# A four-layer decoder trunk on one core: the issue order of all five queues from a fixed table

## The chip, the core and the metric

The kernel runs on one core of a Trainium2 chip. The core has five instruction queues that run side by side and meet through semaphores: TensorE (PE) for matmuls and transposes, VectorE (DVE), ScalarE (ACT) and GpSimd (POOL) for elementwise work, and SyncE (SP), which here only issues DMAs. Each queue works through its instructions in the order in which the program has them; an instruction that waits holds everything behind it on its queue. The metric is device time in microseconds of one execution; the profile is one such execution, recorded instruction by instruction.

## What is computed

One sequence of 1024 positions, width 1024, goes through four layers, causal, all positions at once. The token mixers are, in order, HGRN2, sliding-window attention, gated DeltaNet and HGRN2 again:

```python
for i in range(DEPTH):
    j = i // N_MIXERS
    mod = (c @ ada_w[i] + ada_b[i])[:, None, :]
    shift, scale, gate = jnp.split(mod, 3, axis=-1)
    h = rmsnorm(x, norm_g[i]) * (1.0 + scale) + shift
    kind = i % N_MIXERS
    if kind == 0:
        y = hgrn2_mixer(h, hg_in_w[j], hg_out_w[j], hg_onorm[j], lb_all[i])
    elif kind == 1:
        y = swa_mixer(h, sw_in_w[j], sw_out_w[j], sw_qnorm[j], sw_knorm[j], sw_sinks[j], ang)
    else:
        y = gdn_mixer(h, gd_in_w[j], gd_out_w[j], gd_conv_w[j], gd_a_log[j], gd_dt_bias[j], gd_onorm[j])
    x = x + gate * y
```

Each mixer is an input projection of width 4096 (HGRN2), 2560 (attention) or 6176 (DeltaNet), a sequence part, a gate and an output projection. The sequence part of HGRN2 is a recurrence in chunks with one 128 x 128 state for each of 8 heads; attention looks back 128 positions with 16 heads; DeltaNet is a recurrence in chunks with 16 value heads, a triangular inverse for each chunk and a short convolution ahead of it. All is float32.

## The kernel before

Activations lie with the 1024 channels on partitions (8 blocks of 128) and the positions in two halves of 512. A float32 product is made of three matmuls of rounded parts: every tile is split into a high part and a remainder, and `mm3` issues high x high (L222), high x low and low x high (L223, L224). Weights come from memory in 256 KB tiles (`load_w`: DMA on SP, cast to the high part on ACT, L193, remainder on DVE, L194). These projection matmuls, 128 x 512 each, are most of PE's work; the tiles they fill in PSUM are called proj_ps, projw_ps, projt_ps and outp_ps, and few of them exist at a time (three, in DeltaNet two), so that ACT and DVE must empty one before it is filled again.

The mixers' sequence parts are chains of small matmuls with ACT or DVE steps between them:

- HGRN2 (`mix` in `hgrn2`): decayed products (lev_ps, L1125 and L1170), a transpose (kh_ps, L1192), then for each of four chunks the output (o_ps, L1202 and L1203) and the next state (s_ps, L1207, which DVE turns into hg_S). The first layer's last head ends in a transpose ot_ps (L1234).
- Attention (`mix` in `swa`): transposes of q (L1481), scores (s_ps, L1496 to L1498), softmax on ACT and DVE, transposes of the weights (pt_ps, L1519, copied by ACT to sw_pth) and the product with v (pv_ps, L1525).
- DeltaNet (`scan` in `gdn`): for each chunk of 128 positions the products of the state with k and q (ks_ps, L942 and L943), gd_y on DVE, w_ps (L953), its scaled copies gd_ws and gd_wg on ACT (L954, L968), S_ps (L958), the new state gd_S on DVE, and w_ps once more (L969). Beside it run the inverse (`inverse`, L790 to L899) and the projections of later heads, whose convolution (`conv`) empties proj_ps by ACT's L692 and L696; transposes of k, q and v (L711) follow, with sums of squares on ACT (L718).

What is issued when is not written out by hand. The functions are generators, and `weave` takes turns between several of them (a recurrence, the projections of later heads, the next layer's adaLN vectors), each in proportion to a total that is written beside it. From what it is given so the framework orders each queue when the program is closed, by priorities (`high_priority`, with offsets such as `PRH` or `BURST`), by data dependencies, and by its own estimate of when an operand is ready. `issue_after` and `tied` add single order edges.

## Time and profile before

| what | value |
| --- | --- |
| median of three runs | 2648.4 us |
| lowest and highest of them | 2642.19 and 2651.18 us |
| the profiled execution | 2641.07 us |
| its span, first to last instruction | 2639.2 us |
| mean granted clock of PE in it | 0.995 |
| memory traffic | 117 GB/s over the span |

The page of the profile gives the busy time of each engine over the span. Further views cut it into windows, list the instructions of one engine in order of time, and name what ended a wait. PE's records overlap: a projection matmul's record is about 0.39 us long where the next begins 0.23 us after it, so short waits of PE don't show as idle time.

### The profile page before, as it was taken

Reading aid. Unit: us, or ns where it says so; the run is one execution under the profiler, and the core shown is the slowest. Engines: PE = TensorE matmul, PEld = TensorE weight load, DVE = VectorE, ACT = ScalarE, POOL = GpSimd, SP = SyncE. Lnnn points to the kernel's source line nnn. Section 1 sums busy time; section 2 is a strip of 40 time slices with the busy share of each in tenths; the row PEclk is TensorE's granted clock in tenths of the full one; section 3 lists DMA queues with packets and bytes.
Section 4 is the critical chain, followed back from the end, with each engine's and each line's share of the span. In section 5 each row is a group of like instructions: output and inputs, shape, how many; then the busy total and the mean of one; then the engine's idle time right before and its main releaser. Section 6 shows DMA issues by size and latency. Waiting matters only on the chain.

```text
span 2639.2 us, 50831 instructions
## 1 busy us (share of the span) xinstructions
PE 2556.0 (97%) x18271; PEld 2037.9 (77%) x18271; DVE 2020.7 (77%) x5663; ACT 1328.6 (50%) x3478; POOL 162.2 (6%) x382
## 2 busy tenths in 40 slices
PE   7999999999999999999999999999999999999999
PEld 4777777788888867777777777778678877787777
DVE  5585789877797878868899999988776837368775
ACT  4343344543464655545666665666544434245452
POOL 0001000001000000101010101110221000000000
PEclk8999999999999999999999999999999999999999
DMA  7333343643233252434343444334585312122443
GB/s 261 96 114 105 109 144 114 192 129 126 66 105 104 71 163 95 141 98 117 104 113 100 110 117 116 81 98 103 181 248 171 116 49 81 46 85 64 144 136 117
DMA packets 393617, 312.06 MB, mean 118 GB/s; under 512 B 74979, under 2 KB 320150, under 8 KB 393366
## 3 DMA queue, kind: packets, MB, share of 16 engines
q1 hardware_dynamic: 380822, 267.92, 34.5%
q0 software_dynamic: 12544, 40.90, 4.9%
q8 instruction: 144, 2.36, 0.4%
q14 instruction: 107, 0.88, 0.1%
HBM read 247.84 MB, written 60.88 MB: 117 GB/s over the span
## 4 chain that ended last, share of the span: by engine, by line
PE 73%; DVE 14%; DMA 6%; ACT 4%; issue 3%; SPq 1%; POOL 0%; DVEq 0%; ACTq 0%; POOLq 0%
PE proj_ps L222 10%; PE proj_ps L224 10%; PE proj_ps L223 10%; PE outp_ps L224 5%; PE outp_ps L222 5%; PE outp_ps L223 5%; PE projw_ps L223 2%; PE projw_ps L222 2%; PE projw_ps L224 2%; DMA ada_w<-in_ada_w_dram 2%; DVE gd_tb L698 1%; DVE w_lo L194 1%; PE projt_ps L223 1%; PE projt_ps L224 1%; PE projt_ps L222 1%
## 5 line engine op out<-in xcount | busy, mean ns | idle before, releaser
L222 PE MATMUL proj_ps<-hhi,w_hi 128*128 128x512 f32 x1664 | 676.0, 407 | 3.6 <-ACT gd_tb L696 3.3
L223 PE MATMUL proj_ps<-hlo,w_hi 128*128 128x512 f32 x1664 | 672.1, 404 | 0.0
L224 PE MATMUL proj_ps<-hhi,w_lo 128*128 128x512 f32 x1664 | 671.3, 404 | 0.0
L222 PEld LDWEIGHTS proj_ps<-hhi,w_hi 128*128 128x128 f32 x1664 | 314.7, 189 | 64.2 <-ACT gd_tb L696 5.9
L224 PEld LDWEIGHTS proj_ps<-hhi,w_lo 128*128 128x128 f32 x1664 | 314.4, 189 | 58.2 <-issue 0.4
L223 PEld LDWEIGHTS proj_ps<-hlo,w_hi 128*128 128x128 f32 x1664 | 315.0, 189 | 55.1 <-issue 0.9
L193 ACT CAST w_hi<-w_raw 128x512 fp32r<-128x512 f32 x356 | 216.7, 612 | 264.9 <-PE proj_ps L223 148.7
L194 DVE TENSOR_TENSOR w_lo<-w_raw,w_hi 128x512 fp32r<-128x512 f32 x356 | 239.1, 676 | 143.3 <-ACT w_hi L193 139.8
L222 PE MATMUL outp_ps<-o_hi,w_hi 128*128 128x512 f32 x576 | 228.3, 397 | 1.1 <-DVE x L1356 1.1
L223 PE MATMUL outp_ps<-o_lo,w_hi 128*128 128x512 f32 x576 | 228.7, 397 | 0.5 <-DVE o_lo L1331 0.4
L224 PE MATMUL outp_ps<-o_hi,w_lo 128*128 128x512 f32 x576 | 227.8, 396 | 0.5 <-DVE w_lo L194 0.5
L196 ACT ACTIVATE w_hi<-w_raw,par 128x512 fp32r<-128x512 f32 (+1 forms) x136 | 94.8, 697 | 141.6 <-PE outp_ps L223 95.0
L698 DVE SCALAR_TENSOR_TENSOR gd_tb<-gd_xs,taps,gd_tb 128x512 f32<-128x512 f32 x192 | 145.8, 759 | 16.3 <-ACT gd_tb L696 12.5
L448 DVE SCALAR_TENSOR_TENSOR ada_acc<-ada_w,par,ada_acc 128x512 f32<-128x512 f32 x154 | 115.0, 746 | 21.7 <-DMA ada_w<-in_ada_w_dram 20.9
L197 DVE SCALAR_TENSOR_TENSOR w_lo<-w_raw,par,w_hi 128x512 fp32r<-128x512 f32 (+1 forms) x136 | 96.8, 715 | 42.7 <-ACT w_hi L196 42.2
L222 PEld LDWEIGHTS outp_ps<-o_hi,w_hi 128*128 128x128 f32 x576 | 108.6, 189 | 24.7 <-issue 2.9
L223 PEld LDWEIGHTS outp_ps<-o_lo,w_hi 128*128 128x128 f32 x576 | 108.6, 189 | 23.4 <-DVE o_lo L1331 1.6
L224 PEld LDWEIGHTS outp_ps<-o_hi,w_lo 128*128 128x128 f32 x576 | 108.5, 188 | 22.9 <-DVE w_lo L194 1.0
L1322 POOL DMA_DIRECT2D o_in<-od x72 | 38.9, 541 | 1194.5 <-DVE sw_zs L1465 334.0
L222 PE MATMUL projw_ps<-w_hi,hhi 128*128 128x512 f32 x256 | 102.5, 406 | 2.4 <-DVE hg_q L1041 2.4
L223 PE MATMUL projw_ps<-w_lo,hhi 128*128 128x512 f32 x256 | 103.5, 406 | 0.3 <-DVE w_lo L194 0.3
L224 PE MATMUL projw_ps<-w_hi,hlo 128*128 128x512 f32 x256 | 102.2, 400 | 0.0
(429 smaller groups left out, 5360.1 us busy)
## 6 DMA issues: line engine op xcount, KB each, us to landing
ada_w<-in_ada_w_dram SPq DMA_DIRECT2D x160, 256.0 KB, 2.8
w_raw<-in_hg_in_w_dram SPq DMA_DIRECT2D x148, 256.0 KB, 2.8
w_raw<-in_gd_in_w_dram SPq DMA_DIRECT2D x128, 256.0 KB, 3.0
o_in<-od POOLq DMA_DIRECT2D x72, 256.0 KB, 3.6
x<-xd SPq DMA_DIRECT2D x64, 256.0 KB, 4.7
w_raw<-in_gd_out_w_dram SPq DMA_DIRECT2D x64, 256.0 KB, 3.3
xd<-x POOLq DMA_DIRECT2D x48, 256.0 KB, 2.8
w_raw<-in_sw_in_w_dram SPq DMA_DIRECT2D x44, 256.0 KB, 2.9
```

Of the source, the lines that this page charges most:

```text
L193: nc.scalar.copy(hi, raw)
L194: nc.vector.tensor_tensor(lo, raw, hi.bitcast(F32), ALU.subtract)
L196: nc.scalar.activation(hi, raw, AF.Copy, scale=scale)
L197: nc.vector.scalar_tensor_tensor(lo, raw, scale, hi.bitcast(F32), ALU.mult, ALU.subtract)
L222: mm(out, a[0], b[0], start=start, stop=False)
L223: mm(out, a[0], b[1], start=False, stop=False)
L224: mm(out, a[1], b[0], start=False, stop=stop)
L448: self.step = self.nc.vector.scalar_tensor_tensor(acc, w, c, acc, ALU.mult, ALU.add)
L698: last = nc.vector.scalar_tensor_tensor(y, xs[:, j:j + HT], w(j), y, ALU.mult, ALU.add)
L1322: nc.gpsimd.dma_start(t, od[(k0 + k) * P:(k0 + k + 1) * P, sl])
```

## The change

A table gives the order of all five queues. `trunk` calls `in_order` as its last step, when all instructions have been written down. For each queue the table holds, in compressed form, which of the instructions left is the next one; `in_order` ties each instruction to the one that the table puts ahead of it on its queue by an order edge, which asks for no wait. Priorities then have nothing left to decide. The table was worked out beforehand with longer hand-overs between engines. Operations, tiles and buffers are the same; only ACT gets two table loads more (8 for 6), which the compiler places where two functions of different tables follow each other.

```diff
+import base64
+import zlib
...
+ORDER = {
+    "PE": (
+        "c-rlo>2nmv6~N!FW>>qqZwawlohu2nI*?!`ap*z<gySF)?1(!7a~KHm2jU2m3J`<{kV>4wI1q4Ta8+W5xSVoTlFzB6Dqr#~Uy}SM`INk)dv>"
...
+    "Activation": (
...
+    "DVE": (
...
+    "SP": (
...
+    "Pool": (
...
+}
+
+
+def in_order(tc):
+
+
+    rest = {}
+    for i in tc.nc.cur_bb.bb.instructions:
+        if type(i).__name__ not in ("BassTilePoolBoundary", "InstRegisterMove"):
+            rest.setdefault(i.engine, []).append(i)
+    for e, table in ORDER.items():
+        left, places, last = rest[getattr(mybir.EngineType, e)], iter(zlib.decompress(base64.b85decode(table))), None
+        for n in places:
+            i = left.pop(n if n < 255 else next(places) + 256 * next(places))
+            if last is not None:
+                how = mybir.DependencyInfo(mybir.DependencyClass.NoSync, mybir.DependencyReason.DATA)
+                tc.add_manual_dep(i, last, how, reason="order")
+            last = i.name
+        assert not left
...
+    in_order(tc)
```

The new lines shift the kernel's line numbers by 128: L222 of before is L350 in rows of the change, L953 is L1081, and so on. On PE, 31% of the instructions keep their place, half move by at most 4 places and nine in ten by at most 25. On SP 51% keep theirs and none moves by more than 19; on POOL none by more than 8.

**First place: PE in the first HGRN2 layer, last head** (about 495 us in the profile of before), where the first chunk's output and state begin. Rows are line, operation, tile written <- tiles read, size. Before:

```order
L1192 MATMUL kh_ps<-ident,hg_kg 128x128 x4
L1203 MATMUL o_ps<-hg_v_513,hg_at_506 128x128
L1207 MATMUL s_ps<-hg_v_513,hg_kht 128x128
L1202 MATMUL o_ps<-hg_S,hg_qf 128x128
L1203 MATMUL o_ps<-hg_v_513,hg_at_506 128x128
L1207 MATMUL s_ps<-hg_v_513,hg_kht 128x128
L224 MATMUL proj_ps<-hhi,w_lo 128x512
```

The same first s_ps and the o_ps that needs its state, in the change:

```order
L1335 MATMUL s_ps<-hg_v_513,hg_kht 128x128
L351 MATMUL proj_ps<-hlo,w_hi 128x512
L352 MATMUL proj_ps<-hhi,w_lo 128x512
L350 MATMUL proj_ps<-hhi,w_hi 128x512
L351 MATMUL proj_ps<-hlo,w_hi 128x512
L352 MATMUL proj_ps<-hhi,w_lo 128x512
L1330 MATMUL o_ps<-hg_S,hg_qf 128x128
L1331 MATMUL o_ps<-hg_v_513,hg_at_506 128x128
L1335 MATMUL s_ps<-hg_v_513,hg_kht 128x128
```

Where o_ps stood right behind the s_ps whose state it needs, five projection matmuls now stand between the two.

**Second place: PE in DeltaNet's recurrence** (about 1293 us), where w_ps, S_ps and ks_ps of one head pair follow each other. Before:

```order
L953 MATMUL w_ps<-gd_y,gd_uq 128x128
L222 MATMUL proj_ps<-hhi,w_hi 128x512
L223 MATMUL proj_ps<-hlo,w_hi 128x512
L224 MATMUL proj_ps<-hhi,w_lo 128x512
L958 MATMUL S_ps<-gd_ws,gd_kt 128x256
L969 MATMUL w_ps<-gd_wg,gd_uq 128x128
L222 MATMUL proj_ps<-hhi,w_hi 128x512
L223 MATMUL proj_ps<-hlo,w_hi 128x512
L224 MATMUL proj_ps<-hhi,w_lo 128x512
L969 MATMUL w_ps<-gd_wg,gd_uq 128x128
```

In the change the same chunk, from the step ahead of it to the next projection matmul:

```order
L1086 MATMUL S_ps<-gd_ws,gd_kt 128x256
L1097 MATMUL w_ps<-gd_wg,gd_uq 128x128 x2
L1070 MATMUL ks_ps<-gd_S,gd_k 128x256
L1071 MATMUL ks_ps<-gd_S,gd_q 128x256
L1081 MATMUL w_ps<-gd_y,gd_uq 128x128 x2
L1086 MATMUL S_ps<-gd_ws,gd_kt 128x256
L1097 MATMUL w_ps<-gd_wg,gd_uq 128x128 x2
L1070 MATMUL ks_ps<-gd_S,gd_k 128x256
L1071 MATMUL ks_ps<-gd_S,gd_q 128x256
L350 MATMUL proj_ps<-hhi,w_hi 128x512
```

Two steps' worth of the recurrence, twelve instructions, now stand together, and the projection matmuls that stood between them stand ahead and behind.

**Third place: ACT in DeltaNet** (about 1396 us), around the sums of squares of q's transposes and the L696 that empties proj_ps. Before:

```order
L949 ACTIVATE gd_qse<-ks_ps,gd_ed 128x128
L718 ACTIVATE gd_tb,gd_ms<-qtr_ps 128x128 x4
L954 ACTIVATE gd_ws<-w_ps,gd_gw 128x128
L968 ACTIVATE gd_wg<-w_ps,gd_gm 128x128
L696 ACTIVATE gd_tb<-proj_ps,taps 128x512
L968 ACTIVATE gd_wg<-w_ps,gd_gm 128x128
```

In the change:

```order
L1082 ACTIVATE gd_ws<-w_ps,gd_gw 128x128
L832 ACTIVATE gd_tb<-gd_tb 128x512
L1096 ACTIVATE gd_wg<-w_ps,gd_gm 128x128 x2
L846 ACTIVATE gd_tb,gd_ms<-qtr_ps 128x128 x4
L824 ACTIVATE gd_tb<-proj_ps,taps 128x512
L1105 ACTIVATE gd_sq,gd_oms<-gd_ot 128x128 x2
```

The four sums (L718, now L846) moved behind gd_ws and both gd_wg, and L696 (now L824) stands right behind them. On PE the q transposes moved from nine rows ahead of the projection matmul that needs this L696 to four rows ahead.

## The prediction

> **What bounds the kernel now.** I read the page first: the busy shares, then the chain that ended last.

> ```profile
> span 2639.2 us, 50831 instructions
> ...
> PE 2556.0 (97%) x18271; PEld 2037.9 (77%) x18271; DVE 2020.7 (77%) x5663; ACT 1328.6 (50%) x3478; POOL 162.2 (6%) x382
> ...
> PE 73%; DVE 14%; DMA 6%; ACT 4%; issue 3%; SPq 1%; POOL 0%; DVEq 0%; ACTq 0%; POOLq 0%
> ```

> TensorE (PE) is busy for 2556.0 of 2639.2 us, and most of the chain is its own matmuls. Every PE instruction stays, so the order can only change the time that PE spends waiting: 83 us are seen as idle. So the next view is busy time by stage, in windows that I cut where the PE instructions of one layer give way to those of the next: set-up, first HGRN2 layer, attention, DeltaNet (GDN), second HGRN2 layer.

> ```profile
> core 0: us, PE busy (x) PEld busy (x) DVE busy (x) ACT busy (x) POOL busy (x), PEclk, DMA share, GB/s
> 0.00:57.00 57.00, 40.82 (x148) 21.52 (x149) 32.60 (x104) 22.67 (x40) 1.12 (x8) 0.88 0.83 302
> 57.00:520.00 463.00, 447.52 (x3921) 353.80 (x3922) 343.76 (x1083) 199.28 (x506) 14.74 (x52) 0.99 0.41 122
> 620.00:990.00 370.00, 361.26 (x2472) 301.64 (x2473) 287.81 (x826) 194.06 (x488) 6.50 (x12) 1.00 0.31 98
> 1240.00:1860.00 620.00, 604.73 (x4481) 484.88 (x4479) 563.71 (x1641) 395.65 (x1255) 54.73 (x138) 1.00 0.41 107
> 2130.00:2510.00 380.00, 375.79 (x3407) 298.12 (x3406) 247.88 (x869) 159.08 (x425) 2.17 (x4) 1.00 0.27 84
> ```

> Window length less PE busy gives the idle time: 16.2 us in the set-up, 15.5 and 4.2 in the two HGRN2 windows, 8.7 in attention, 15.3 in GDN. VectorE (DVE) is busy for 563.71 of 620 us in GDN (91%) and for 74%, 78% and 65% in the other three. There is little spare on DVE in GDN, and more elsewhere.

> The last view is the timeline of PE, for the price of one hand-over: PE writes PSUM, ACT or DVE reads it and writes SBUF, and a later matmul needs that. First a covered one, then an uncovered one (a plain fp32 matmul leaves two records, x2).

> ```profile
> 1285.78 0.39 PE L969 MATMUL w_ps<-gd_wg,gd_uq 128*128 128x128 f32 x2
> 1285.92 0.47 PE L222 MATMUL proj_ps<-hhi,w_hi 128*128 128x512 f32 x1
> 1286.23 0.39 PE L223 MATMUL proj_ps<-hlo,w_hi 128*128 128x512 f32 x1
> 1286.45 0.40 PE L224 MATMUL proj_ps<-hhi,w_lo 128*128 128x512 f32 x1
> 1286.76 0.49 PE L969 MATMUL w_ps<-gd_wg,gd_uq 128*128 128x128 f32 x2
> ...
> 1883.51 0.38 PE L969 MATMUL w_ps<-gd_wg,gd_uq 128*128 128x128 f32 x2
> 1884.35 0.49 PE L969 MATMUL w_ps<-gd_wg,gd_uq 128*128 128x128 f32 x2 [0.46 <-ACT gd_wg L968]
> ```

> With three projection matmuls between the two L969, the second starts 0.98 us after the first and nothing idles. With none it starts 0.84 us after it. The first occupies PE for 0.14 (1285.78 to 1285.92), so 0.70 us of PE time is lost. A projection matmul takes 0.22 to 0.31 (1285.92, 1286.23, 1286.45); I take 0.23. So a hand-over loses **0.70 us with no projection matmul in between, 0.47 with one, 0.24 with two and nothing with three**. Only part of it shows as idle, since records overlap (0.39 long, 0.23 apart).

> **The change, part by part.** The five queues hold the same instructions on the same buffers in another order; ACT has two table loads more. So each term is a count of hand-overs times that price. For every matmul of the mixers that waits for ACT or DVE, I followed its wait back in both orders to the last PE instruction that it needs, and counted the projection matmuls between the two.

> *HGRN2, both layers.* Matmuls with none, one or two in between: 16, 6 and 56 before; 7, 2 and 19 now. The first place of the section on the change is one of them. Before: 16 x 0.70 + 6 x 0.47 + 56 x 0.24 = 27.4 us. Now: 4.9 + 0.9 + 4.6 = 10.4. The change is **-17**. The same place shows a dearer hand-over, through DVE:

> ```profile
> 495.60 0.49 PE L1207 MATMUL s_ps<-hg_v,hg_kht 128*128 128x128 f32 x2
> 496.64 0.46 PE L1202 MATMUL o_ps<-hg_S,hg_qf 128*128 128x128 f32 x2 [0.56 <-DVE hg_S L1210]
> ```

> From 495.60 to 496.64 are 1.04 us, so 0.90 less the matmul's 0.14; at 0.90, 0.67 and 0.44 the same counts give 43.0 and 16.0, a gain of 27. The other end is nothing, if what releases these matmuls simply arrives later. I keep 0 to -27 and take 17, because it agrees with the 19.7 us of idle time in the two windows.

> *The longest single wait of that stage.*

> ```profile
> PE ot_ps L1234 <- DVE hg_tmp L1230: 2.8, 1, 2.8
> ...
> 508.00:511.50 3.50, 2.87 (x9) 2.52 (x10) 1.85 (x4) 1.32 (x3) 0.00 (x0) 0.51 0.19 56
> ```

> PE waits 2.8 us for hg_tmp, and the granted clock in the 3.5 us behind it is 0.51, so about 1.7 us more is lost there. In the new order six more projection matmuls stand ahead of that transpose, 6 x 0.23 = 1.4 us. That leaves a wait of 1.4 and, I assume, a clock that stays up: **-3** (0 to -4.5).

> *Attention.* 8, 7 and 2 before; 2, 4 and 5 now. 9.4 us before, 4.5 now: **-5** (0 to -9, the idle time of its window).

> *GDN.* Here the count goes the other way: 33, 20 and 17 before; 55, 16 and 29 now. 36.6 us before, 53.0 now: **+16**. Two patterns make it, shown at the second and third place of the section on the change. The first: chunk steps of the recurrence (L942, L943, L953, L958, L969) that follow each other with no projection matmul between. Runs of five or more such instructions: one of 13 before, in and around the window 1876 to 1884 us, and six now, of 12, 5, 8, 12, 6 and 14. The one of before shows what a run is:

> ```profile
> 1880.52 0.49 PE L953 MATMUL w_ps<-gd_y,gd_uq 128*128 128x128 f32 x2 [1.36 <-DVE gd_y L948]
> ...
> 1876.00:1884.00 8.00, 4.67 (x23) 3.22 (x22) 4.41 (x11) 5.47 (x20) 1.60 (x3) 1.00 0.29 94
> ```

> PE is busy for 4.67 of 8 us there. What waits behind the waiting instruction on PE are the projection matmuls of the next heads; ACT's and DVE's convolutions wait for these. The second pattern is on ACT:

> ```profile
> 1396.29 0.28 ACT L718 ACTIVATE gd_tb<-qtr_ps 128x128 f32<-128x128 f32 x1 [0.35 <-PE qtr_ps L711]
> ...
> 1397.06 0.29 ACT L718 ACTIVATE gd_tb<-qtr_ps 128x128 f32<-128x128 f32 x1
> ...
> 1397.81 0.73 ACT L696 ACTIVATE gd_tb<-proj_ps,taps 128x512 f32<-128x512 f32 x1
> ```

> A projection matmul that starts a new PSUM tile needs L696, which empties that tile, and L696 stands behind four L718 that need the transposes of q. The four take about 1.0 us (three steps from 1396.29 to 1397.06 are 0.77), L696 0.73. Of the L222 that wait for an L696, four had up to three projection matmuls of cover before, and ten have now. Six more at up to 1.5 us would be +9; I take none of it beyond the count, since some of these waits stand behind another wait that already lets ACT catch up. The bounds of GDN are 0 (PE would wait elsewhere in a stage where DVE is 91% busy) and +40, worked out under the rivals.

> *Table loads.*

> ```profile
> L1038 ACT ACT_TABLE_LOAD x3 | 3.8, 1283 | 0.1
> ```

> The second rope sine (L394) now stands behind sigmoids and squares, so its table is loaded again: 2 x 1.28 us on ACT, in the first HGRN2 window, where ACT is busy for 199 of 463 us and its casts run ahead of PE. Taken as 0 (0 to +2.6, if a gate that PE waits for stands behind a load).

> *DMA queues.* About half of SP's instructions keep their place and none moves by more than 19; GpSimd's move by 8 at most.

> ```profile
> PE ada_row L432 <- DMA ada_w<-in_ada_w_dram: 6.4, 2, 5.5
> ...
> w_raw<-in_gd_in_w_dram SPq DMA_DIRECT2D x128, 256.0 KB, 3.0
> ```

> PE's long wait for a transfer is that of the set-up, where the order hardly changes; the weight tiles, landing in 3.0 us, are issued ahead. Taken as 0 (-3 to +3).

> **Sum.** -17 - 3 - 5 + 16 = **-9 us**. The profiled execution took 2641.1 us (its span and 1.9 around it) and would take 2632. It lies 7.3 below the median of the three runs, 2648.4, so on the median's scale the forecast is **2639**, 0.35% less. About 0.3% (8 us) is what a measurement of this kernel can tell from no change, so this forecast lies at the edge.

> **Rivals.**

> *GDN gets the upper hand: slower.* The uncovered runs wait for DVE as at 1880.52 (1.36 us) rather than 0.70, because gd_y stands behind the inverse and the convolutions in DVE's own order. The 22 new uncovered hand-overs then cost 22 x 0.66 = 15 us more, and the six L222 the 9 us above: GDN +40. With -25 elsewhere that is +15, **2663**. It decides once GDN costs over 33. For: DVE's 91%. Against: in such a run PE feeds DVE nothing new, so DVE should catch up.

> *GDN costs nothing.* PE's waits there only change places, since DVE sets the pace: -25, **2623**. For: the same 91%. Against: PE is busy for 604.73 of 620 us too, and what it loses in a run it has no spare time to regain.

> *Nothing changes.* The 28 us of idle time in HGRN2 and attention is given back because the releasing ACT and DVE instructions moved back as well: **2648**. Against: the places shown have the matmuls moved by more than the wait.

> *The clock drops in the new runs.* Five new runs with one stretch of 3.4 us at half clock each, as behind 508 us, cost 5 x 1.7 = 8.5 us: **2647**. Against: the clock is 1.00 in 1876 to 1884 although PE idles for 3.3 of 8 us. [...]

> **How the numbers follow.** The forecast gets 0.45: its terms are rough, so 0.24 of it is faster by over 0.3%, 0.17 within, 0.04 slower. GDN for nothing 0.17, all faster. Nothing changes 0.12, all within. The clock 0.06, within but for 0.01 slower. GDN upper hand 0.20: 0.17 slower, 0.03 within. Together 0.41 faster, 0.37 within 0.3%, 0.22 slower. The range goes from 2616 (GDN free and HGRN2 at nearly 27) to 2664 (the slower rival), which leaves about a tenth out on each side.

> **What would show it.** In the changed profile, idle PE time in the first HGRN2 window should fall from 15.5 to about 6 us, in attention from 8.7 to about 5, and in GDN rise from 15.3 to some 25 or 30. In GDN's timeline the six runs should show S_ps, w_ps and ks_ps with idle time before them, released by gd_ws, gd_wg, gd_S and gd_y. If HGRN2 stays at 15, the hand-over count was the wrong measure; if GDN stays at 15, DVE sets its pace; if the granted clock falls in GDN, the last rival holds.

## Result and profile after

The changed kernel takes 2628.20 us (median of 4 runs, 2624.95 to 2630.06), the kernel before 2646.53 beside it (4 runs, 2642.19 to 2651.18). The ratio is **0.9929, 95% interval 0.9908 to 0.9950**, 18 us less. A second measurement, among the experiments, gave 0.9935 (0.9917 to 0.9954). The forecast was 2639 with a range from 2616 to 2664. On the scale of the profiled executions it was 2632; the profiled execution of the change took 2630.06 us, of which the span is 2628.4.

The page of the changed kernel: span, busy times, and the chain that ended last by engine.

```profile
span 2628.4 us, 50793 instructions
...
PE 2542.7 (97%) x18271; PEld 2058.0 (78%) x18271; DVE 2014.9 (77%) x5663; ACT 1328.7 (51%) x3480; POOL 164.7 (6%) x382
...
PE 80%; DVE 7%; DMA 6%; issue 4%; ACT 3%; SPq 0%; POOL 0%; DVEq 0%; ACTq 0%; POOLq 0%
```

VectorE's share of the chain has halved (14% before), TensorE's has grown from 73 to 80%: less of the span hangs on a hand-over. Busy time by stage, in the same windows as before (length, then busy time and records of each engine, granted clock, DMA share, GB/s):

```profile
0.00:57.00 57.00, 41.96 (x150) 22.89 (x151) 32.55 (x104) 23.06 (x41) 1.11 (x8) 0.84 0.84 302
57.00:520.00 463.00, 450.68 (x3960) 359.97 (x3960) 347.11 (x1094) 204.14 (x515) 14.77 (x52) 0.99 0.41 125
620.00:990.00 370.00, 366.50 (x2510) 311.17 (x2509) 289.48 (x830) 197.52 (x494) 6.61 (x13) 0.99 0.32 100
1240.00:1860.00 620.00, 592.08 (x4208) 483.41 (x4208) 548.51 (x1599) 386.79 (x1234) 53.52 (x132) 0.99 0.39 101
2130.00:2510.00 380.00, 378.71 (x3472) 304.45 (x3471) 254.19 (x885) 163.97 (x438) 3.24 (x6) 1.00 0.28 88
```

Idle TensorE time (length less busy) goes from 15.5 to 12.3 us in the first HGRN2 window, from 8.7 to 3.5 in attention, from 4.2 to 1.3 in the second HGRN2 window, and in GDN from 15.3 to **27.9**. The windows are fixed in time and the stages have moved in them, so I also took the start of every PE instruction in both traces (they are the same instructions) and the median difference, change less before, in stretches of 30 us: -10.3 us at 540, -20.3 at 1200, +1.0 at 1920, -10.9 at 2610. Stage by stage that is **-10 in the first HGRN2 layer, -10 in attention, +21 in GDN, -12 from there to the end**. For GDN the windows can be cut at the same instructions, which gives 5065 PE records in both (before, then the change):

```profile
1220.12:1940.10 719.98, 698.89 (x5065) 558.39 (x5064) 641.22 (x1805) 457.54 (x1426) 81.06 (x187) 1.00 0.44 118
1199.30:1941.10 741.80, 704.69 (x5065) 573.91 (x5064) 645.84 (x1820) 456.23 (x1426) 83.68 (x187) 0.98 0.42 114
```

The stage is 21.8 us longer. 16.0 us of it is idle time (21.1 to 37.1), and 5.8 us is longer busy time of the same matmuls.

The waits of TensorE on the instructions of GDN (us in total, times, longest), of the kernel before and then of the change (its lines are 128 higher: L696 is now L824, L953 is L1081):

```profile
PE proj_ps L222 <- ACT gd_tb L696: 3.3, 4, 1.5
...
PE S_ps L958 <- ACT gd_ws L954: 1.4, 3, 0.6
PE w_ps L953 <- DVE gd_y L948: 1.4, 1, 1.4
...
PE w_ps L969 <- ACT gd_wg L968: 1.2, 2, 0.8
```

```profile
PE proj_ps L350 <- ACT gd_tb L824: 9.9, 10, 1.6
...
PE proj_ps L350 <- DVE gd_tb L918: 4.8, 2, 2.4
PE w_ps L1081 <- DVE gd_y L1076: 3.9, 5, 0.9
...
PE S_ps L1086 <- ACT gd_ws L1082: 3.0, 6, 0.6
...
PE w_ps L1097 <- ACT gd_wg L1096: 2.6, 6, 0.6
PE w_ps L1081 <- ACT gd_ws L1082: 2.5, 5, 0.5
PE ks_ps L1070 <- DVE gd_S L1092: 2.3, 3, 1.2
```

Both patterns of the prediction are there: the waits of the recurrence, and the projection matmul behind L696, with the ten places that were counted; it is now the largest of TensorE's waits. A third one has come up that the prediction did not have: a projection matmul waits for a step of the inverse on VectorE (L918, which is L790 of before, where the wait is 0.2), 2.3 us ahead of GDN and 2.4 in it, at 1222 us. One of the six crowded runs in the change's timeline (start, length, engine, line, tile; idle time before it and what ended it):

```profile
1280.30 0.49 PE L1097 MATMUL w_ps<-gd_wg,gd_uq 128*128 128x128 f32 x2 [0.61 <-ACT gd_wg L1096]
1280.63 0.60 PE L1070 MATMUL ks_ps<-gd_S,gd_k 128*128 128x256 f32 x2
1281.06 0.59 PE L1071 MATMUL ks_ps<-gd_S,gd_q 128*128 128x256 f32 x2
1282.58 0.49 PE L1081 MATMUL w_ps<-gd_y,gd_uq 128*128 128x128 f32 x2 [0.92 <-DVE gd_y L1076]
1283.53 0.49 PE L1081 MATMUL w_ps<-gd_y,gd_uq 128*128 128x128 f32 x2 [0.46 <-ACT gd_ws L1082]
1284.47 1.22 PE L1086 MATMUL S_ps<-gd_ws,gd_kt 128*128 128x256 f32 x2 [0.46 <-ACT gd_ws L1082]
```

S_ps takes 1.22 us here and 0.70 elsewhere (x2 records, 1278.78): the clock has halved. The windows around it, cut where the clock changes:

```profile
1281.09:1284.50 3.41, 1.57 (x8) 0.79 (x6) 3.27 (x12) 2.18 (x9) 0.00 (x0) 1.00 0.41 103
1284.50:1291.33 6.83, 6.31 (x16) 4.99 (x17) 5.79 (x19) 3.58 (x17) 0.00 (x0) 0.50 0.17 42
```

TensorE is busy for 1.57 of 3.41 us, never idle for more than 0.92 us in one go, and the next 6.83 us run at half clock. The prediction had given this a chance of 0.06.

Why runs of this kind arise can be read from the number of projection matmuls between the ks_ps pair and the w_ps that waits for gd_y (the cover of that wait), for chunk steps 4 to 7 of the first and third head groups (u=0 and u=2):

```
              step 4   step 5   step 6   step 7
before  u=0      3        6        2        4
change  u=0      5       35        0        7
before  u=2      5       16        9       16
change  u=2      5       39        0       16
```

In the change VectorE's queue has 7.4 us of other work (the inverse, norms, transposes, convolutions) between the ks_ps pair of step 5 and its gd_y; the table covers this wait with 35 to 39 projection matmuls, and none are left for step 6.

### The profile page after: what moved, and what is told of

The parts are those of the page before. It is cut to its first block, busy times and chain, and to the rows that moved or that the text cites. A ratio compares the mean times of both kernels' runs of the same rounds, so it can differ in the third digit from the quotient of the medians.

```text
span 2628.4 us, 50793 instructions
## 1 busy us (share of the span) xinstructions
PE 2542.7 (97%) x18271; PEld 2058.0 (78%) x18271; DVE 2014.9 (77%) x5663; ACT 1328.7 (51%) x3480; POOL 164.7 (6%) x382
## 4 chain that ended last, share of the span: by engine, by line
PE 80%; DVE 7%; DMA 6%; issue 4%; ACT 3%; SPq 0%; POOL 0%; DVEq 0%; ACTq 0%; POOLq 0%
PE proj_ps L350 12%; PE proj_ps L351 12%; PE proj_ps L352 12%; PE outp_ps L350 4%; PE outp_ps L351 4%; PE outp_ps L352 4%; PE projw_ps L352 2%; PE projw_ps L351 2%; PE projw_ps L350 2%; DMA ada_w<-in_ada_w_dram 2%; PE projt_ps L350 2%; PE projt_ps L351 2%; PE projt_ps L352 2%; PE lev_ps L1253 1%; PE pv_ps L1653 1%
## 5 line engine op out<-in xcount | busy, mean ns | idle before, releaser
L350 PE MATMUL proj_ps<-hhi,w_hi 128*128 128x512 f32 x1664 | 677.0, 407 | 16.4 <-ACT gd_tb L824 9.9
L350 PEld LDWEIGHTS proj_ps<-hhi,w_hi 128*128 128x128 f32 x1664 | 315.2, 190 | 80.2 <-ACT gd_tb L824 15.6
L350 PE MATMUL outp_ps<-o_hi,w_hi 128*128 128x512 f32 x576 | 228.4, 398 | 1.6 <-ACT o_hi L1458 1.0
L350 PEld LDWEIGHTS outp_ps<-o_hi,w_hi 128*128 128x128 f32 x576 | 108.7, 189 | 25.0 <-issue 2.5
L350 PE MATMUL projw_ps<-w_hi,hhi 128*128 128x512 f32 x256 | 101.6, 402 | 2.4 <-DVE hg_q L1169 2.3
## 6 DMA issues: line engine op xcount, KB each, us to landing
ada_w<-in_ada_w_dram SPq DMA_DIRECT2D x160, 256.0 KB, 2.8
w_raw<-in_hg_in_w_dram SPq DMA_DIRECT2D x148, 256.0 KB, 2.9
w_raw<-in_gd_in_w_dram SPq DMA_DIRECT2D x128, 256.0 KB, 3.0
o_in<-od POOLq DMA_DIRECT2D x72, 256.0 KB, 3.6
x<-xd SPq DMA_DIRECT2D x64, 256.0 KB, 4.8
w_raw<-in_gd_out_w_dram SPq DMA_DIRECT2D x64, 256.0 KB, 3.2
xd<-x POOLq DMA_DIRECT2D x48, 256.0 KB, 2.7
w_raw<-in_sw_in_w_dram SPq DMA_DIRECT2D x44, 256.0 KB, 3.0
```

Of the source, the lines that this page charges most:

```text
L350: mm(out, a[0], b[0], start=start, stop=False)
```

## Experiments

Most of them mix the two orders. The order of before is written as a second table of the same form; the program is cut into pieces at places of the order of before, in all five queues at once and so that no piece needs a later one; within each piece either order is followed. TAKE names the pieces that follow the table of the change.

```diff
+TAKE = [0, 1, 3]
...
+def mixed(e):
+    now, was = places(ORDER[e]), places(WAS[e])
+    piece = {n: sum(k >= c for c in CUTS[e]) for k, n in enumerate(was)}
+    rank = {n: k for k, n in enumerate(now)}, {n: k for k, n in enumerate(was)}
+    return sorted(was, key=lambda n: (piece[n], rank[piece[n] not in TAKE][n]))
```

### Stage by stage

Cuts at 560, 1220 and 1940 us of the trace of before, which make four pieces: set-up with the first HGRN2 layer, attention, GDN, the second HGRN2 layer with the end.

All but GDN (TAKE = [0, 1, 3]):

> The order of the change in set-up, both HGRN2 layers and attention, the order of before in DeltaNet (GDN). By matching the same PE instructions in the two traces, the change gained about 10 us in the first HGRN2 layer, 10 in attention and 11 from the second HGRN2 layer to the end, and lost about 21 in GDN. Theory (each stage's gain and loss is its own): the 21 us of GDN stay away, so -31 us against before, about 1.2% (ratio 0.988). Rival (GDN starts earlier and then waits for something that the earlier stages do not bring nearer, so the loss is the earlier gain given back): GDN gives back 20 us in the old order too, ratio as the change's, 0.993 or nearer to 1.

GDN alone (TAKE = [2]):

> The order of the change in GDN alone, the order of before elsewhere. Theory: GDN's order costs what the two traces show there, +21 us (ratio 1.008), with idle PE time in the window of GDN up from 15 to about 28 us and the granted clock down to 0.5 for some stretches of 3.4 us. By the prediction's sum it would be +16 (1.006). Rival (gain given back): no gain ahead of it, so nothing to give back, 0 (ratio 1.000).

HGRN2 alone (TAKE = [0, 3]):

> The order of the change in set-up and in both HGRN2 layers (the second with what follows to the end), the order of before in attention and GDN. Theory: -21 us (ratio 0.992), idle PE time in the first HGRN2 window down from 15.5 to 12 us and in the second from 4.2 to 1.3. By the prediction's sum -20. Rival (hand-overs are no measure: what releases the matmuls comes later as well): within 0.2% of before.

Attention alone (TAKE = [1]):

> The order of the change in attention and the feed-forward behind it alone. Theory: -10 us (ratio 0.996), idle PE time in the attention window from 8.7 to some 4 us. By the prediction's sum -5 (0.998). Rival: 0, if the 10 us in the trace of the change were one execution's chance or came from starting earlier.

Measured, each against runs of before taken beside them (2644.86 us):

| order of the change in | ratio | 95% interval | us |
|---|---|---|---|
| all but GDN | 0.9899 | 0.9881 to 0.9918 | -26.7 |
| GDN alone | 1.0082 | 1.0069 to 1.0095 | +21.7 |
| HGRN2 alone | 0.9919 | 0.9905 to 0.9933 | -21.4 |
| attention alone | 0.9981 | 0.9969 to 0.9993 | -5.0 |

HGRN2 and GDN came out as the first theory said, and GDN costs 21.7 us with no gain ahead of it that could be given back, so its rival falls. All but GDN lies between its theory (0.988) and its rival (0.993), nearer to the theory; its interval holds neither. Attention gave 5 us, as the prediction's sum has it, not the 10 seen in place. And the three parts sum to -21.4 - 5.0 + 21.7 = -4.7 us, while the change makes -18: something is not additive. The same comparison of PE starts says where attention's other 5 us went: with its order alone the shift is -7.0 us at 1200 and -1.0 at 1260, at the entrance of GDN; in all but GDN it goes from -21.7 to -15.1 over the same place. There TensorE waits, in the kernel with all but GDN (its lines are 247 above those of before):

```profile
PE ktr_ps L958 <- DVE gd_k L952: 5.2, 1, 5.2
```

The kernel before waits 0.9 us for that tile. Attention's gain brings TensorE to the entrance earlier, and VectorE not by as much: with attention's order alone TensorE starts 6.9 us earlier than before at 1190 us and 7.0 at 1200, VectorE 4.3 and 1.7. To be early is not what costs: with HGRN2's order alone both engines are 5.6 us early at 1200, the wait for that tile is 1.1 us, and 5.4 us of the gain are still there at 1260. In all but GDN, VectorE's queue holds 17 short steps of the first inverse, 5 us in all, between the last two steps of the convolution that ends in gd_k (start, length):

```profile
1197.70 0.28 DVE L1092 TENSOR_TENSOR gd_tmp<-gd_A,gd_Tb 128x120 f32<-128x120 f32 x1
...
1202.45 0.22 DVE L1092 TENSOR_TENSOR gd_tmp<-gd_A,gd_Tb 128x56 f32<-128x56 f32 x1
1202.59 0.74 DVE L945 SCALAR_TENSOR_TENSOR gd_tb<-gd_xs,taps,gd_tb 128x512 f32<-128x512 f32 x1
...
1204.15 0.68 DVE L952 SCALAR_TENSOR_TENSOR gd_k<-gd_tb 128x512 f32<-128x512 f32 x1
```

### One crowded run, another seam, and the change again

Cuts at 1270 and 1940 us with the change outside (late cut, TAKE = [0, 2]); cuts at 1270 and 1320 us with the change inside (first run alone, TAKE = [1]); the change as it is.

> The order of the change in all that stands before 1270 us of the trace of before (set-up, first HGRN2 layer, attention, and the first 50 us of GDN) and again from 1940 us on, the order of before in between. The run with GDN left out as a whole, from 1220 us, lost 6 us at its seam: PE waited 3.4 us there, with 6.8 us at half clock behind it. Theory (that loss belongs to the seam, and GDN's order costs only from the first crowded run at 1305 us on): -33 us against before, ratio 0.9875. Rival (the old order of GDN needs what the old order ahead of it prepares, wherever the seam is): 0.990 again.

> The order of before, but for the piece from 1270 to 1320 us of its trace, which has the order of the change: the first of the six runs, 12 rows of the recurrence with no projection matmul between them. Theory: this one run carries the loss that the trace of the change shows there, +9 us (ratio 1.0035): 8 uncovered hand-overs x 0.70 = 5.6 us, and 6.8 us at half clock = 3.4. By the prediction's forecast, without the clock, +5.6 (1.002). Rival (PE's waits only change places within GDN, as DVE sets its pace): by the end of GDN the loss is made up, 1.000.

> The change itself once more, beside the runs of before of this call, since the three parts run one by one add up to -21.4 - 5.1 + 21.7 = -5 us and the change measured -18 with an interval of 11 us. Theory (stages add up but for what happens at the seams, some 6 to 10 us at the two ends of GDN): -10 to -15 us, ratio 0.995. Rival (the parts help each other): -18 or more, 0.993 or less.

Measured, against 2648.44 us: late cut **0.9910** (0.9891 to 0.9929), first run alone **1.0032** (1.0020 to 1.0045), the change **0.9935** (0.9917 to 0.9954).

The first run costs 8.5 us by itself (5.3 to 11.9), and the loss isn't made up later. The hand-overs with the clock (9) fit, but the 5.6 us without the clock lie inside the interval as well, and the trace of this run shows something that neither sum had: two waits behind L696, 2.2 us together, against 0.2 before in that stretch. So this run doesn't settle the clock's part. The late cut was a miss: it can't be told from all but GDN, and its PE starts lose as much at the entrance, ahead of its seam (-19.9 us at 1200, -14.1 at 1260). So the 6 us are no matter of the seam but of TensorE's being there ahead of VectorE. The change again is -17 us, so the parts do help each other, by some 13 us (with about 7 of uncertainty). From the PE starts, about half of that lies at the entrance: TensorE's lead costs 7 us there with the old order of GDN, the first run 9 us without that lead (3.6 to 12.8 us in GDN alone), and in the change both together cost 10 (-20.3 at 1200, -9.9 at 1380). The two losses overlap, in the same 100 us. The rest is no larger than the intervals allow for and stays open.

### The entrance of GDN

> The run with GDN left out (ratio 0.9899), with one place of TensorE's queue altered: the four ktr_ps transposes at GDN's entrance, which wait 5.2 us for gd_k at 1199 us, stand 19 projection matmuls (19 x 0.23 = 4.3 us) further back; the other four queues are as they were. Theory (attention arrives early and the wait at the entrance gives it back, since nothing is left ahead of those four): 4 us of the wait and the 3.4 us of the halved clock behind it go, -7 us, ratio 0.987. Rival (VectorE paces the entrance, so the wait turns up at the next matmul that needs VectorE): 0.990 as before.

```diff
         order = mixed(e)
+        if e == "PE":
+            order = [n for n in order if n not in [6842, 6843, 6844, 6845]]
+            k = order.index(6885) + 1
+            order[k:k] = [6842, 6843, 6844, 6845]
```

Measured **0.9878** (0.9853 to 0.9903) against 2648.70 us; all but GDN had 0.9899 (0.9881 to 0.9918), so the two can't be told apart. The waits in the same place say which theory holds:

```profile
PE qtr_ps L962 <- DVE gd_q L956: 4.3, 1, 4.3
PE ktr_ps L962 <- DVE gd_k L956: 1.2, 2, 0.9
```

The wait for gd_k fell from 5.2 us to 1.2 in two places, and 4.3 us turned up at the next transposes, which wait for gd_q. So the wait moves, as the rival says. That VectorE sets the pace is shown for gd_k, ahead of which its queue runs without a wait. Ahead of gd_q it has one:

```profile
1210.17 0.72 ACT L947 ACTIVATE gd_tb<-proj_ps,taps 128x512 f32<-128x512 f32 x1
...
1210.97 0.75 DVE L949 SCALAR_TENSOR_TENSOR gd_tb<-gd_xs,taps,gd_tb 128x512 f32<-128x512 f32 x1 [2.06 <-DMA tblk<-gd_Tb]
```

The convolution that ends in gd_q starts with L947 on ACT, which stands behind the copy and the sums of the very transposes that were moved back, and ends 0.08 us before VectorE's L949 starts; the profile puts the wait down to a transfer of the inverse that landed at the same time. Which of the two decided isn't shown. Either way, moving four instructions of TensorE's queue alone moved the wait and didn't end it.

### The clock

> The run with GDN's order alone, plus 15 matmuls whose results are never used (an fp32 128x128 by 256 columns each, 0.43 us in the trace): two ahead of the w_ps matmul that waits for gd_y in five chunk steps without a projection matmul, and one ahead of the second matmul that waits for gd_wg in five. They add no hand-over and take none away; they only keep TensorE busy while it waits, so that the 3.4 us around it are busy for over 0.65 instead of 0.46 to 0.55. Theory (half of GDN's +21.7 us is the halved clock behind such stretches): the two stretches of 6.8 and one of 3.4 us at half clock at 1310, 1904 and 1494 go, some 6 to 8 us, ratio 1.0055 against 1.0082. Rival (the clock plays no part; hand-overs and DVE do it all): the same 1.008, or slower by up to 15 x 0.43 = 6.5 us where the fillers stand in the way, 1.0105.

```diff
                     pks = self.psum("s", "ks_ps", 1)
+                    if (u, n) in FILL_W:
+                        FILL.setdefault(w1.ins.name, []).append(nc.tensor.matmul(pks[:, 0:256], dd["k"][hf][:, cs], dd["k"][hf][:, 0:256], start=True, stop=True).ins.name)
...
                 wg, ws = f256("wg"), f256("ws")
+                more = [nc.tensor.matmul(po[:, 256:512], dd["k"][hf][:, cs], dd["k"][hf][:, 0:256], start=True, stop=True).ins.name for _ in range(2 * ((u, n) in FILL_Y))]
```

Measured **1.0071** (1.0050 to 1.0091), against 1.0082 (1.0069 to 1.0095) without the fillers: inconclusive as a time. What they did to the waits and the clock isn't: TensorE's waits for gd_y went from 4.0 to 0.5 us and those for gd_wg from 2.6 to 0.6, and none of the stretches at half clock at 1310, 1494 and 1904 us is left. The filled step, with the two fillers (w_ps<-gd_k, x4) in place of a wait of 0.9 us:

```profile
1308.06 0.59 PE L1197 MATMUL ks_ps<-gd_S,gd_q 128*128 128x256 f32 x2
1308.49 1.03 PE L1205 MATMUL w_ps<-gd_k 128*128 128x256 f32 x4
1309.57 0.49 PE L1208 MATMUL w_ps<-gd_y,gd_uq 128*128 128x128 f32 x2
1310.52 0.49 PE L1208 MATMUL w_ps<-gd_y,gd_uq 128*128 128x128 f32 x2 [0.46 <-ACT gd_ws L1211]
```

The mean granted clock of the runs went from 0.9884 to 0.9900.

> The run with GDN left out (ratio 0.9899), plus 59 fp32 matmuls of 128x128 by 128 (the identity by itself, never used, about 0.14 us each) that fill four long waits of TensorE: 12 ahead of the matmul that waits 2.2 us for sw_zs at 606 us, 10 and 7 ahead of those that wait 1.9 us for mod and 1.3 us for sw_qhi at 930 to 934, 30 ahead of the four that wait 5.2 us for gd_k at 1199. They shorten no wait; they keep TensorE busy in it. Theory (a 3.4 us stretch in which TensorE is busy for less than about half halves the clock of the next): the stretches at half clock at 610, 934 and 1204 go, 1.7 + 3.4 + 3.4 = 8.5 us in the profiled execution of the run without them and some 6 in the mean, ratio 0.9875, granted clock up from 0.991 to 0.993 or more. Rival (the halved clock costs nothing there, or is set by something else than how busy TensorE is): 0.990, granted clock unchanged.

```diff
+WARM = {3325: ('s', 12), 5531: ('o', 10), 5539: ('o', 7), 6842: ('s', 30)}
...
+                pt = k.psum(tag, "warm_ps", 2 if tag == "lev" else 1)
+                FILL[n] = [mm(pt[:, 0:128], k.ident, k.ident, start=True, stop=True).ins.name for _ in range(count)]
```

Windows of all but GDN, cut at its clock changes, and the same windows with the fillers:

```profile
606.46:609.88 3.42, 1.26 (x8) 1.06 (x9) 2.06 (x4) 2.16 (x5) 0.00 (x0) 1.00 0.44 146
609.88:613.29 3.41, 3.41 (x19) 3.41 (x17) 1.59 (x3) 1.17 (x3) 0.00 (x0) 0.51 0.69 222
930.79:934.20 3.41, 0.60 (x4) 0.36 (x4) 2.46 (x8) 2.08 (x5) 0.42 (x1) 1.00 0.32 93
934.20:941.03 6.83, 6.72 (x23) 5.60 (x24) 5.71 (x14) 4.73 (x9) 2.36 (x6) 0.50 0.67 214
```

```profile
606.46:609.88 3.42, 3.42 (x33) 3.42 (x31) 2.08 (x3) 1.26 (x2) 0.03 (x1) 1.00 0.85 270
609.88:613.29 3.41, 3.18 (x26) 2.83 (x25) 2.64 (x5) 2.72 (x5) 0.00 (x0) 1.00 0.24 69
930.79:934.20 3.41, 3.41 (x28) 3.20 (x26) 0.62 (x2) 1.15 (x3) 0.00 (x0) 1.00 0.91 287
934.20:941.03 6.83, 5.89 (x44) 5.17 (x42) 5.90 (x16) 4.47 (x9) 2.15 (x4) 1.00 0.49 149
```

Matmuls that compute nothing of use took TensorE's busy time from 1.26 to 3.42 us in the stretch at 606.46 and from 0.60 to 3.41 in the one at 930.79, and the clock behind them is 1.00 where it was 0.51 and 0.50: in these two places it goes by how busy TensorE is. The mean granted clock rose from 0.9908 to 0.9935, which is 0.0027 x 2617 = 7 us less lost to it. The time is **0.9877** (0.9855 to 0.9898), against 0.9899 (0.9881 to 0.9918): 6 us better at face value, with an uncertainty of about 7, so no change isn't excluded. VectorE's queue is the same in both kernels, so its starts can be compared: relative to all but GDN the kernel with the fillers gains 1.1 us between 606 and 612 (expected 1.7), 1.2 between 928 and 960 (expected 3.4) and 1.4 at the entrance of GDN (expected 3.4), and gives up to 2.7 back within GDN. Of the 8.5 us expected, 3.7 came at the three places. That a halved clock costs its full price only where nothing but TensorE is late in what follows is my estimate from these numbers; it was not tried by itself.

> Both: the four ktr_ps transposes 19 projection matmuls further back, and the 29 fillers at 606 and 930 to 934. If both theories hold and add up: -7 from the entrance, -4 from the clock of the two other places, ratio 0.9855, about 38 us less than before. If only the entrance counts 0.987, if only the clock 0.988.

Measured **0.9881** (0.9859 to 0.9904): a miss. The two don't add up, nor is either told from all but GDN; the three kernels took 2618.49, 2617.76 and 2618.35 us and all but GDN 2618.91. All four beat both the kernel before and the change (by some 10 us, with 2628.20 and 2629.87 for the change), and the simplest, the order of the change everywhere but in GDN, is the version to keep.

## Why the prediction was right, and where it was not

| term | forecast, us | measured, us |
|---|---|---|
| HGRN2, with the wait for ot_ps | -17 - 3 | -21.4 (-25 to -18), alone |
| attention | -5 | -5.0 (-8 to -2), alone |
| GDN | +16 | +21.7 (18 to 25) alone, +8 to +10 beside the others (0.9929 and 0.9935 less 0.9899, each with some 7 us of uncertainty) |
| sum | -9 | -18 and -17 |

**HGRN2 held as a sum.** The count of uncovered hand-overs times 0.70, 0.47 and 0.24 us gave -17, and the wait for ot_ps (2.8 us before) is gone from the change's waits, with the half clock behind it (0.51 in 508.00 to 511.50 us before; 1.00 in the change from 62.50 to 612.05). No run takes single hand-overs apart, so the price is supported by the sum alone. The sign named for it didn't come: idle TensorE time in the first window was to fall to about 6 us and fell to 12.3, while the layer got 10 us shorter. The sign was at odds with the prediction's own price, of which only part shows as idle (0.46 of 0.70 us at 1884.35). The records in the window say it better: 3960 instead of 3921, 39 projection matmuls more, 39 x 0.23 = 9 us of work more in the same time.

**Attention held as a time**, as far as an interval of -8 to -2 can tell, by two errors of the count that cancel: the stage gains 10 us in place, and half is lost again at the entrance of GDN, where VectorE isn't ready. The prediction priced each stage by itself and had no term for what TensorE meets when it gets ahead of another engine.

**GDN was mis-sized, and its clock step was wrong.** The recurrence's count held: its waits show 11.5 us more idle time (5.9 to 17.4 in the groups of the page), and by the row at 1884.35 the 22 new uncovered hand-overs would show 22 x 0.46 = 10. What failed is "Six more at up to 1.5 us would be +9; I take none of it beyond the count": the ten L222 behind L696 wait 9.9 us where the four waited 3.3, so 6.6 us belonged in the sum, as did the 2.4 us of the wait for the inverse. Some 4 us shrank elsewhere (vtr_ps from 2.9 to 0.2, z_ps from 7.9 to 6.5). 11.5 + 6.6 + 2.4 - 4 = 16.5 is about the 16.0 us of idle time that the stage gained.

The other step that failed is that the forecast has no half clock in GDN: waits of 0.92, 0.46 and 0.46 us in the 3.41 us from 1281.09 left TensorE busy for 1.57 of them, and the clock of the next 6.83 is 0.50. The window 1876 to 1884, with its clock of 1.00, was no proof against it: TensorE is busy for 4.67 of 8 us there, 58%, and of the 98 stretches with a share from 0.50 to 0.66, 22 had half clock behind them and 76 had not (last section). What this costs in GDN stays open. With GDN alone the mean granted clock is 0.9884 against 0.9920, (0.9920 - 0.9884) x 2662 = 10 us at full price. But the busy time of the stage's matmuls grew by only 5.8 us, and the hidden part of 22 hand-overs, 22 x 0.24 = 5, lies in that too; the fillers, which took nearly half of that clock back (0.9900), left the time where it was within the intervals. The slower rival (uncovered runs at 1.36 us each) didn't come: the longest of the five waits for gd_y is 0.9.

**The sum** missed by 8 to 9 us on the median's scale, -9 against -18 and -17, and that is GDN's term: beside the others it costs 8 to 10 us where 16 stood, since, as far as the trace shows it, its loss and the loss at its entrance overlap; about half of the difference stays open. The range (2616 to 2664) was wide enough to hold GDN at nothing as well as at twice the 16. On the scale of the profiled executions the forecast looks better than it was, 2632 against 2630.06. That is luck: before was profiled at a granted clock of 0.995 where its later runs have 0.992 in the mean (0.003 x 2640 = 8 us), while 2630.06 was the longest of the change's four.

**Rivals.** "Nothing changes" and "GDN costs nothing" fall by the runs of the stages. DMA queues and the two table loads were taken as nothing and no view shows otherwise; neither was tried alone.

## What to carry to other kernels

Count for each wait how much independent work stands between it and what it needs, but count it over the whole stage: work spent on covering one long wait (35 matmuls at step 5) is missing at the next (none at step 6), and several short waits close together can be followed by a halved clock (0.92, 0.46 and 0.46 us within 3.41 at 1281.09, and 0.50 in the 6.83 us behind them). Then ask which engine sets the pace at the entrance of the next stage; what TensorE alone gains ahead of a stage that waits for VectorE is given back there (-7.0 us at 1200, -1.0 at 1260 with attention's order alone), and what both gain is kept (5.6 us at 1200, 5.4 at 1260 with HGRN2's order alone). A table that is good in some stages and bad in others can be taken by stages: all of this one but its GDN piece saves 27 us instead of 18.

## What the hardware showed that was not expected

```
busy share        stretches    next at half clock
below 0.50            48              48
0.50 to 0.66          98              22
0.66 and above      9356               1
```

The longest gap in the stretch ahead of 1284.50 us was 0.92 us, and TensorE was busy for 1.57 of its 3.41 us, 46%.

Most of the scatter between runs goes with the granted clock: the eleven runs with attention's order alone go from 2634.28 us at a mean granted clock of 0.994 to 2648.57 at 0.988, 14.3 us where the clock makes 0.006 x 2640 = 16.
